# Interleaving the last three MLP block products by row tile, with row statistics on ScalarE and small steps on GpSimd

## The chip, the cores and the metric

The kernel runs on one core of a Trainium2 chip. Its engines are TensorE (matrix products into PSUM banks), VectorE, ScalarE and GpSimd (element work), and SyncE, which issues the transfers. Each engine works through a queue of its own in order and waits there for what other engines have to finish first. The metric is the device time of one execution in microseconds; less is better.

## The reference, cut to what matters

One inference step of a one-layer encoder over 1024 prompt rows and 64 sample rows, 1024 wide, in float32. What the change touches is its last line:

```
hdn = square(relu(x @ w_ff1))                          # hidden 4096
y   = layer_norm(alpha * x + hdn @ w_ff2, ln2_g, ln2_b)
layer_norm(x, g, b): mu = mean(x); var = mean((x - mu)**2)     # over the 1024 columns of a row
                     (x - mu) * rsqrt(var + 1e-5) * g + b
```

## The kernel before

The product `hdn @ w_ff2` is done as seven block products in the manner of Strassen and Winograd (P1 to P7) instead of eight, over four groups `g` of the hidden dimension. Each product is a step `s` of a group; each step has four row tiles `t` of 128 prompt rows, and one row tile is one call of `tile_mm`: twelve matmuls of 512 columns (four slices of the hidden dimension, each in three passes of split numbers) into one PSUM bank, then one VectorE instruction (L1306) that adds the bank into `acc`. This addition is called the eviction here. `acc[row]` holds the 1024 columns of row tile `row` (0 to 7; `NB` = 8 is the sample). `QUAD` says which half of the rows and which half of the columns a product belongs to.

Products share banks: P6, P7 and P4 go on accumulating in the bank that P1 began (`a0` to `a3`, one for each `t`), P3 in that of P5 (`b0` to `b3`). So P4 of a tile can't start before the eviction of P7 of the same tile has read the bank. In the last group the order of the steps is P1, P2, P6, P5, P3, P7, P4; steps 4, 5 and 6, that is P3, P7 and P4, finish the rows: rows 0 to 3 are complete after P3, rows 4 to 7 after P4.

TensorE's order is written by hand, here as a list of (step, tile). The order on the other engines is drawn up before the run by a planner that knows the instructions' inputs and estimates of their durations; it is fixed in the program.

`final(row)` normalises a complete row tile and writes it out. Its row statistics come from VectorE: `half_stats` (L1316) over each 512 columns, and an aggregate (L1373). `rstd_of` (L151 to L161) makes the reciprocal root: Ln and Exp on ScalarE, refined by four small VectorE steps on one column. For rows 0 to 5 and the sample, a further small step (L1384) makes the negated mean times root, ScalarE's Identity (L1388) writes the normalised half into a free `b` bank, VectorE multiplies by the gain (L1389), GpSimd adds the bias (L1390), SP issues the transfer. Rows 6 and 7 are done on VectorE alone, by two instructions over the row (L1376, L1379 in halves).

The sample's products (`sample_mm`) run between tiles, in banks `b0` or `b3`; `sample_sum` puts them together.

## Time and profile before

| what | us |
|---|---|
| median of 3 runs | 1297.64 |
| lowest and highest run | 1296.21, 1300.37 |
| the profiled execution | 1297.02 |
| its span, from the first to the last instruction | 1295.2 |
| TensorE busy in the span | 1209.0 (93%) |
| VectorE busy in the span | 952.1 (74%) |
| ScalarE, GpSimd busy in the span | 528.4 (41%), 107.0 (8%) |

Busy shares are means over the whole span. The change touches its last few per cent, so the views that count are those of single stretches there: busy time of each engine in a window, and the engines' timelines. Times in rows are microseconds from the start of the span, unless marked ns. PE is TensorE, PEld its weight loads, DVE VectorE, ACT ScalarE, POOL GpSimd, SPq SyncE's queue. A clock in a row is TensorE's granted clock as a share of 2.4 GHz.

### The profile page before, as it was taken

What the parts mean: (1) busy time and instruction counts of PE and PEld (TensorE: products, weight loads), DVE (VectorE), ACT (ScalarE), POOL (GpSimd) and SP (SyncE); (2) the same over time, 40 slices, a digit from 0 to 9 for tenths busy, and PEclk for the clock granted to TensorE, in tenths of its full rate; (3) what the DMA queues carried; (4) which work ended last, traced back from release to release, by engine and by line L of the source; (5) the groups of instructions that cost most, each with busy time, mean ns of one, the idle gap of its engine ahead of it and who ended that gap; (6) DMA issues with size and microseconds to landing.
All of it is one profiled execution on the core that took longest, in us unless ns stands there. A gap on an engine that the chain in (4) does not pass through costs nothing.

```text
span 1295.2 us, 18517 instructions
## 1 busy us (share of the span) xinstructions
PE 1209.0 (93%) x7162; PEld 1097.0 (85%) x7162; DVE 952.1 (74%) x1635; ACT 528.4 (41%) x1010; POOL 107.0 (8%) x57
## 2 busy tenths in 40 slices
PE   7989899989999799976999999999989999999994
PEld 5889789988899688865999999999978888888873
DVE  7855765866966687799776767676575688777888
ACT  4454464664664442223333333333434423323422
POOL 3130111111110010011000000000000000000013
PEclk9999899989999899987999999999989999999997
DMA  7771231222222443323535353542695545434203
GB/s 249 236 209 38 39 99 55 52 63 79 59 59 88 59 132 123 119 81 106 181 109 179 104 178 113 168 139 94 228 342 210 195 160 177 143 130 144 68 17 121
DMA packets 123234, 166.61 MB, mean 129 GB/s; under 512 B 13885, under 2 KB 90729, under 8 KB 119562
## 3 DMA queue, kind: packets, MB, share of 16 engines
q1 hardware_dynamic: 123146, 165.43, 40.6%
q8 instruction: 56, 0.92, 0.3%
q14 instruction: 32, 0.26, 0.1%
HBM read 112.20 MB, written 55.57 MB: 130 GB/s over the span
## 4 chain that ended last, share of the span: by engine, by line
PE 71%; DVE 16%; DMA 5%; ACT 4%; issue 4%; SPq 1%; DVEq 0%; POOL 0%; ACTq 0%; POOLq 0%
PE P L1299 19%; PE py L839 6%; PE fa L1001 5%; PE fa L999 5%; PE fa L997 5%; PE fc L999 2%; PE fc L997 2%; PE fc L1001 2%; PE v L480 1%; PE fb L999 1%; PE fb L997 1%; PE fb L1001 1%; DMA wo6r<-in_w_out 1%; PE t L644 1%; PE smP L1337 1%
## 5 line engine op out<-in xcount | busy, mean ns | idle before, releaser
L1299 PE MATMUL P<-wl,hh 128*128 128x512 f32 x448 | 175.7, 392 | 3.1 <-DVE wl L1150 3.1
L1299 PE MATMUL P<-wh,hh 128*128 128x512 f32 x448 | 175.6, 392 | 1.0 <-DVE sacc L1343 0.8
L1299 PE MATMUL P<-wh,hl 128*128 128x512 f32 x448 | 175.6, 392 | 0.0
L1299 PEld LDWEIGHTS P<-wl,hh 128*128 128x128 f32 x448 | 84.8, 189 | 21.2 <-DVE wl L1150 3.4
L1299 PEld LDWEIGHTS P<-wh,hh 128*128 128x128 f32 x448 | 84.8, 189 | 19.5 <-DVE sacc L1343 1.2
L1299 PEld LDWEIGHTS P<-wh,hl 128*128 128x128 f32 x448 | 84.8, 189 | 17.7
L1306 DVE TENSOR_TENSOR x<-x,P 128x512 f32<-128x512 f32 x96 | 64.4, 682 | 34.0 <-PE P L1299 33.7
L1148 ACT CAST hh<-hr 128x1024 fp32r<-128x1024 f32 (+1 forms) x28 | 37.2, 1359 | 110.2 <-PE P L1299 105.3
L997 PE MATMUL fc<-x,wP 128*128 128x272 f32 x248 | 71.6, 289 | 2.2 <-ACT x L203 2.2
L999 PE MATMUL fc<-x,wP 128*128 128x272 f32 x248 | 71.7, 289 | 0.8 <-DVE x L204 0.8
L1001 PE MATMUL fc<-x,wP 128*128 128x272 f32 x248 | 71.3, 288 | 0.0
L1390 POOL TENSOR_TENSOR x<-x 128x1024 f32<-128x1024 f32 x6 | 14.3, 2381 | 671.9 <-DVE n21v L156 656.9
L1150 DVE TENSOR_TENSOR hl<-hr,hh 128x1024 fp32r<-128x1024 f32 (+1 forms) x28 | 44.7, 1603 | 31.5 <-ACT hh L1148 31.5
L997 PEld LDWEIGHTS fc<-x,wP 128*128 128x128 f32 x248 | 46.7, 188 | 2.4 <-ACT x L203 2.4
L999 PEld LDWEIGHTS fc<-x,wP 128*128 128x128 f32 x248 | 46.8, 189 | 1.0 <-DVE x L204 1.0
L1001 PEld LDWEIGHTS fc<-x,wP 128*128 128x128 f32 x248 | 46.8, 189 | 0.0
L1001 PE MATMUL fa<-x,wP 128*128 128x272 f32 x128 | 38.1, 298 | 6.2 <-DVE wP L204 6.2
L619 PE MATMUL s<-kh,qs 128*128 128x512 f32 (+3 forms) x96 | 35.1, 369 | 7.0 <-DVE a20m L565 2.6
L1148 ACT CAST hh<-x 128x1024 fp32r<-128x1024 f32 (+1 forms) x13 | 17.6, 1384 | 53.3 <-PE P L1299 40.1
L997 PE MATMUL fa<-x,wP 128*128 128x272 f32 x128 | 38.0, 297 | 1.2 <-ACT wP L203 1.2
L999 PE MATMUL fa<-x,wP 128*128 128x272 f32 x128 | 37.8, 295 | 0.0
L203 ACT CAST x<-xt 128x512 fp32r<-128x512 f32 (+2 forms) x33 | 16.8, 545 | 49.2 <-PE xt L908 31.4
(1462 smaller groups left out, 3856.6 us busy)
## 6 DMA issues: line engine op xcount, KB each, us to landing
hr<-hv SPq DMA_DIRECT2D x19, 1024.0 KB, 4.9
hv<-hS SPq DMA_DIRECT2D x63, 256.0 KB, 4.4
w2B<-in_w_ff SPq DMA_DIRECT2D x11, 1024.0 KB, 5.7
hv<-hb SPq DMA_DIRECT2D x42, 256.0 KB, 2.9
x<-hv SPq DMA_DIRECT2D x9, 1024.0 KB, 5.5
f1r<-in_w_ff SPq DMA_DIRECT2D x17, 512.0 KB, 4.1
f1k<-in_w_ff SPq DMA_DIRECT2D x14, 512.0 KB, 4.9
x<-in_w_ff SPq DMA_DIRECT2D x6, 1024.0 KB, 7.6
```

Source lines behind the costliest of these rows:

```text
L203: nc.scalar.copy(out=hi, in_=src)
L480: nc.tensor.matmul(pv, lhsT=xx[:, k, off:off + 128], rhs=ww[:, k, :], start=(n == 0), stop=(n == len(ops) - 1))
L619: nc.tensor.matmul(p[:, c0:c1], lhsT=st, rhs=kh[:, m, c0:c1], start=True, stop=False)
L839: nc.tensor.matmul(py[:, s], lhsT=(ml if m == 2 else mh)[:, e, :], rhs=wo[e][m == 1][:, s], start=(n == 0), stop=(n == len(ops) - 1))
L997: nc.tensor.matmul(out, lhsT=w[:, 0, k, :], rhs=xh[:, k, cs], start=first and k == 0, stop=False, skip_group_check=not first)
L999: nc.tensor.matmul(out, lhsT=w[:, 0, k, :], rhs=xl[:, k, cs], start=False, stop=False, skip_group_check=not first)
L1001: nc.tensor.matmul(out, lhsT=w[:, 1, k, :], rhs=xh[:, k, cs], start=False, stop=last and k == 3, skip_group_check=not first)
L1148: nc.scalar.copy(out=hi[q], in_=src[:, w * q:w * q + w])
L1150: nc.vector.tensor_tensor(out=lo[q], in0=src[:, w * q:w * q + w], in1=f32(hi[q]), op=ALU.subtract)
L1299: nc.tensor.matmul(out, lhsT=x[f][:, c], rhs=w[f], start=new and f == 0 and n == 0, stop=f == GP - 1 and n == 2, skip_group_check=not new)
L1306: nc.vector.tensor_tensor(out=dst, in0=dst, in1=out, op=ALU.add)
L1390: nc.gpsimd.tensor_tensor(out=y[:rows], in0=y[:rows], in1=b, op=ALU.add)
```

## The change

Four things change. First, TensorE's list: P7 and P4 no longer follow all of P3, but the three steps are interleaved so that rows of the two halves become complete in turn; each (6,t) comes directly behind (5,t). `ready_rows` says after which tile which rows are normalised. Second, the rows below `SUMMED` = 6 no longer get statistics from `half_stats`: their evictions are made by `tensor_tensor_reduce`, which also gives the sum of each row, and ScalarE makes the squared deviations' sum by Square with a bias (the negated mean) and an accumulator. Third, the small one-column steps of these six rows and of the sample (`eng`) go to GpSimd; they lie as columns `c[n]` in one tile. Fourth, rows 6 and 7 keep `half_stats` and VectorE's small steps, but are now normalised by ScalarE's Identity too; their bias is added by GpSimd in halves (row 6) or by VectorE (row 7), and each half is written out by itself.

```diff
--- before.py
+++ after.py
@@ -1300,22 +1300,36 @@
                                      stop=f == GP - 1 and n == 2, skip_group_check=not new)
             half, dh = QUAD[p]
             dst = acc[4 * half + t][:, dh * 512:(dh + 1) * 512]
+            row = 4 * half + t
             if g == 0 and p in FIRST:
                 nc.scalar.copy(out=dst, in_=out)
+            elif g == NG - 1 and p in LAST_OF and row < SUMMED:
+                nc.vector.tensor_tensor_reduce(out=dst, in0=out, in1=dst, op0=ALU.add, op1=ALU.add, scale=1.0, scalar=0.0,
+                                               accum_out=col(row, dh))
             else:
                 nc.vector.tensor_tensor(out=dst, in0=dst, in1=out, op=ALU.add)
-            if g == NG - 1 and p in ("P2", "P7"):
-                half_stats(4 * half + t, dh)
+                if g == NG - 1 and p in LAST_OF:
+                    half_stats(row, dh)
+
+
+        LAST_OF = ("P2", "P3", "P7", "P4")
+        SUMMED = 6
+        kept2 = []
+
+        def stat_tile():
+            if not kept2:
+                kept2.append(f1a.tile([128, 1128], F32, name="n2st", tag="wx", bufs=2))
+            return kept2[0]
+
+        def col(t, n):
+            return stat_tile()[:, 128 + 16 * t + n:129 + 16 * t + n]
+
+        def stats_of(t):
+            return stat_tile()[:, 12 * t:12 * t + 12].rearrange("p (q c) -> p q c", q=2)
 
         def half_stats(t, q):
             rows = 128 if t < NB else SMP
-            if not stats2:
-                both = f1a.tile([128, 1128], F32, name="n2st", tag="wx", bufs=2)
-                for u in range(NB + 1):
-                    stats2[u] = both[:, 12 * u:12 * u + 12].rearrange("p (q c) -> p q c", q=2)
-            nc.vector.bn_stats(out=stats2[t][:rows, q, :], in_=acc[t][:rows, q * 512:(q + 1) * 512])
-
-        stats2 = {}
+            nc.vector.bn_stats(out=stats_of(t)[:rows, q, :], in_=acc[t][:rows, q * 512:(q + 1) * 512])
 
         def sample_sum(q):
 
@@ -1367,28 +1381,47 @@
             rows = 128 if t < NB else SMP
             dst = o["y_prompt"][0, t * 128:(t + 1) * 128, :] if t < NB else o["y_sample"][0]
             g, b = gb2[:rows, 0], gb2[:rows, 1]
-            if t < NB:
-                half_stats(t, 1 if t < 4 else 0)
-            mv = small([128, 2], f"n2{t}mv")
-            nc.vector.bn_aggr(out=mv[:rows], in_=stats2[t][:rows])
             halves = [slice(0, 512), slice(512, 1024)]
-            if t >= NB - 2 and t < NB:
-                nc.vector.scalar_tensor_tensor(out=y, in0=y, scalar=mv[:, 0:1], in1=g, op0=ALU.subtract, op1=ALU.mult)
-                r = rstd_of(mv[:, 1:2], rows, f"n2{t}")
-                for s in halves:
-                    nc.vector.scalar_tensor_tensor(out=y[:, s], in0=y[:, s], scalar=r, in1=b[:, s], op0=ALU.mult, op1=ALU.add)
+            if t < 4:
+                xn = [ps2.tile([128, 512], F32, name=f"xn{t}", tag=f"b{t}")] * 2
+            else:
+                xn = [ps2.tile([128, 512], F32, name=f"xn{t}{q}", tag=f"b{2 * (t == 6) + q}") for q in range(2)]
+            c = [col(t, n)[:rows] for n in range(16)]
+            late = SUMMED <= t < NB
+            eng = nc.vector if late else nc.gpsimd
+            if t < SUMMED:
+                eng.tensor_scalar(out=c[2], in0=c[0], scalar1=c[1], scalar2=-1.0 / D, op0=ALU.add, op1=ALU.mult)
+                for q, s in enumerate(halves):
+                    nc.scalar.activation(out=xn[q][:rows], in_=y[:rows, s], func=AF.Square, bias=c[2], scale=1.0,
+                                         accum_out=c[3 + q])
+                eng.tensor_scalar(out=c[5], in0=c[3], scalar1=c[4], scalar2=1.0 / D, op0=ALU.add, op1=ALU.mult)
+                var, mean, sign = c[5], c[2], 1.0
+            else:
+                mv = stat_tile()[:rows, 128 + 16 * t + 11:128 + 16 * t + 13]
+                nc.vector.bn_aggr(out=mv, in_=stats_of(t)[:rows])
+                var, mean, sign = mv[:, 1:2], mv[:, 0:1], -1.0
+            nc.scalar.activation(out=c[6], in_=var, func=AF.Ln, bias=eps[:rows], scale=1.0)
+            nc.scalar.activation(out=c[7], in_=c[6], func=AF.Exp, scale=-0.5)
+            eng.tensor_scalar(out=c[8], in0=var, scalar1=EPS, scalar2=None, op0=ALU.add)
+            eng.tensor_scalar(out=c[8], in0=c[8], scalar1=c[7], scalar2=c[7], op0=ALU.mult, op1=ALU.mult)
+            eng.tensor_scalar(out=c[8], in0=c[8], scalar1=-0.5, scalar2=1.5, op0=ALU.mult, op1=ALU.add)
+            eng.tensor_scalar(out=c[9], in0=c[8], scalar1=c[7], scalar2=None, op0=ALU.mult)
+            eng.tensor_scalar(out=c[10], in0=mean, scalar1=c[9], scalar2=sign, op0=ALU.mult, op1=ALU.mult)
+            for q, s in enumerate(halves):
+
+                nc.scalar.activation(out=xn[q][:rows], in_=y[:rows, s], func=AF.Identity, scale=c[9], bias=c[10])
+                if t == NB - 1:
+                    nc.vector.tensor_tensor(out=xn[q], in0=xn[q], in1=g[:, s], op=ALU.mult)
+                    nc.vector.tensor_tensor(out=y[:, s], in0=xn[q], in1=b[:, s], op=ALU.add)
+                else:
+                    nc.vector.tensor_tensor(out=y[:rows, s], in0=xn[q][:rows], in1=g[:, s], op=ALU.mult)
+                    if late:
+                        nc.gpsimd.tensor_tensor(out=y[:, s], in0=y[:, s], in1=b[:, s], op=ALU.add)
+                if late:
                     nc.sync.dma_start(out=dst[:, s], in_=y[:, s])
-                return
-            r = rstd_of(mv[:rows, 1:2], rows, f"n2{t}")
-            nmr = small([128, 1], f"n2{t}nm")
-            nc.vector.tensor_scalar(out=nmr[:rows], in0=mv[:rows, 0:1], scalar1=r[:rows], scalar2=-1.0, op0=ALU.mult, op1=ALU.mult)
-            for q, s in enumerate(halves):
-
-                xn = ps2.tile([128, 512], F32, name=f"xn{t}{q}", tag=f"b{t if t < 4 else 2 * (t % 2) + q}")
-                nc.scalar.activation(out=xn[:rows], in_=y[:rows, s], func=AF.Identity, scale=r[:rows], bias=nmr[:rows])
-                nc.vector.tensor_tensor(out=y[:rows, s], in0=xn[:rows], in1=g[:, s], op=ALU.mult)
-            nc.gpsimd.tensor_tensor(out=y[:rows], in0=y[:rows], in1=b, op=ALU.add)
-            nc.sync.dma_start(out=dst, in_=y[:rows])
+            if not late:
+                nc.gpsimd.tensor_tensor(out=y[:rows], in0=y[:rows], in1=b, op=ALU.add)
+                nc.sync.dma_start(out=dst, in_=y[:rows])
 
         steps = [(g, s) for g in range(NG) for s in range(7)]
         for n, (g, s) in enumerate(steps):
@@ -1414,17 +1447,14 @@
             if s in (0, 1, 5):
                 sample_mm(g, s)
         g = NG - 1
-        for s, t in ((4, 0), (4, 1), (4, None), (4, 2), (4, 3), (5, 0), (5, 1), (5, 2), (6, 0), (5, 3), (6, 1), (6, 2), (6, 3)):
+        ready_rows = {(4, None): (0, 1), (6, 0): (NB, 4), (4, 2): (2,), (6, 1): (5,), (4, 3): (3,), (6, 2): (6,), (6, 3): (7,)}
+        for s, t in ((4, 0), (4, 1), (4, None), (5, 0), (6, 0), (4, 2), (5, 1), (6, 1), (4, 3), (5, 2), (6, 2), (5, 3), (6, 3)):
             if t is None:
                 sample_mm(g, s)
-                final(0)
-                final(1)
-                continue
-            tile_mm(g, s, t)
-            if s == 6 or (s == 4 and t > 1):
-                final(t if s == 4 else 4 + t)
-            if (s, t) == (4, 3):
-                final(NB)
+            else:
+                tile_mm(g, s, t)
+            for row in ready_rows.get((s, t), ()):
+                final(row)
 
 
 _INS = ["x_prompt", "x_sample", "cache_k", "cache_v", "cache_conv", "ln0_g", "ln0_b", "rel_bias", "w_in", "conv_w",
```

## Rows read from the trace of the kernel before

**Rows 1.** By stretch: length; PE, PEld, DVE, ACT, POOL busy; clock; DMA share, GB/s

```profile
1237.00:1249.00 12.00, 10.42 (x45) 8.29 (x46) 9.61 (x13) 3.80 (x3) 0.00 (x0) 1.00 0.00 0
1249.00:1276.60 27.60, 27.58 (x121) 22.32 (x119) 25.84 (x70) 10.99 (x24) 12.02 (x5) 1.00 0.19 77
1276.60:1292.20 15.60, 0.00 (x0) 0.00 (x0) 14.29 (x27) 3.80 (x9) 4.68 (x2) 0.58 0.34 118
```

**Rows 2.** TensorE's timeline: start, us, engine, line, operation, tiles [idle before <-releaser]

```profile
1235.92 0.39 PE L1299 MATMUL P<-wh,hl 128*128 128x512 f32 x1
1237.07 0.50 PE L1299 MATMUL P<-wh,hh 128*128 128x512 f32 x1 [0.77 <-DVE sacc L1343]
...
1247.04 0.50 PE L1337 MATMUL smP<-wh,hs 128*128 128x512 f32 x1 [1.51 <-DVE x L1306]
...
1276.19 0.39 PE L1299 MATMUL P<-wh,hl 128*128 128x512 f32 x1
```

**Rows 3.** Timeline of VectorE, one eviction and the tail

```profile
1236.34 0.68 DVE L1343 TENSOR_TENSOR sacc<-sacc,smP 128x512 f32<-128x512 f32 x1
...
1275.61 1.64 DVE L1376 SCALAR_TENSOR_TENSOR x<-x,n26mv 128x1024 f32<-128x1024 f32 x1
...
1277.30 0.67 DVE L1306 TENSOR_TENSOR x<-x,P 128x512 f32<-128x512 f32 x1
1278.00 0.69 DVE L1316 BATCH_NORM_STATS2 n2st<-x 128x6 f32<-128x512 f32 x1
...
1279.86 0.20 DVE L1373 BATCH_NORM_AGGREGATE n27mv<-n2st 128x2 f32<-128x12 f32 x1
...
1280.24 3.14 DVE L1376 SCALAR_TENSOR_TENSOR x<-x,n27mv 128x1024 f32<-128x1024 f32 x1
...
1283.73 0.21 DVE L1384 TENSOR_SCALAR n25nm<-n25mv,n25q 128x1 f32<-128x1 f32 x1
1284.80 0.69 DVE L1389 TENSOR_TENSOR x<-xn,x 128x512 f32<-128x512 f32 x1 [0.85 <-ACT xn L1388]
...
1286.85 2.98 DVE L1379 SCALAR_TENSOR_TENSOR x<-x,n26q 128x512 f32<-128x512 f32 x2
...
1289.99 0.27 DVE L156 TENSOR_SCALAR n27v<-n27v,n27r 128x1 f32<-128x1 f32 x1
...
1290.74 1.42 DVE L1379 SCALAR_TENSOR_TENSOR x<-x,n27q 128x512 f32<-128x512 f32 x2
```

**Rows 4.** One line, an earlier normalisation: count: ns min/median/max, first and last start

```profile
L196 DVE SCALAR_TENSOR_TENSOR xn<-xn,n02q,b x1: 1285/1285/1285, 25.3 to 25.3; 128x1024 f32<-128x1024 f32 x1
```

**Rows 5.** Timeline of GpSimd in the tail

```profile
1279.97 2.34 POOL L1390 TENSOR_TENSOR x<-x 128x1024 f32<-128x1024 f32 x1 [3.80 <-DVE n25v L155]
1286.27 2.34 POOL L1390 TENSOR_TENSOR x<-x 128x1024 f32<-128x1024 f32 x1 [3.97 <-DVE x L1389]
```

**Rows 6.** VectorE by line, 1249.0 to 1292.2: count, busy us, mean ns, idle

```profile
L1316 DVE BATCH_NORM_STATS2 n2st<-x 128x6 f32<-128x512 f32 x10 | 6.9, 687 | 0.1
```

**Rows 7.** Line 565, an addition with a reduction, attention stage

```profile
L565 DVE CUSTOM_DVE_ANT_0 a03e<-s,bias x2: 693/693/693, 111.5 to 121.3; 128x512 f32<-128x512 f32 x2
L565 DVE DVE_READ_ACCUMULATOR2_ANT a03m<- x2: 83/84/84, 112.2 to 121.9; 128x1 f32 x2
```

**Rows 8.** Line 568, ScalarE's Exp with a sum, attention stage

```profile
L568 ACT ACTIVATE a03e<-a03e,a03m x2: 727/727/727, 112.3 to 122.1; 128x512 f32<-128x512 f32 x2
```

**Rows 9.** Timeline of ScalarE in the tail

```profile
1283.98 1.49 ACT L1388 ACTIVATE xn<-x,n25nm,n25q 128x512 f32<-128x512 f32 x2 [4.78 <-DVE n25nm L1384]
...
1285.50 0.28 ACT L151 ACTIVATE n27l<-n27mv,eps 128x1 f32<-128x1 f32 x1
1285.82 0.20 ACT L153 ACTIVATE n27r<-n27l 128x1 f32<-128x1 f32 x1
```

**Rows 10.** GpSimd by line, whole span: count, busy us, mean ns, idle before

```profile
masks.py:199 POOL TENSOR_SCALAR_AFFINE_SELECT ident<-ident 128x128 f32<-128x128 f32 x1 | 0.3, 285 | 0.0
...
L1457 POOL MEMSET const-float32-0.0<- 128x1 f32 x1 | 0.1, 99 | 0.2 <-issue 0.2
```

## The prediction

> **What bounds the kernel now.** I read the windows over the last 60 us first [rows 1], because the change touches only the end of the MLP's last group. From 1249.0 to 1276.6 TensorE is busy 27.58 of 27.60 us at a granted clock of 1.00 (2.4 GHz). Then it does nothing more, while VectorE is busy 14.29 of the next 15.60 us. So the end of this kernel is two bounds in a row: TensorE up to its last matmul, and behind it a VectorE backlog. The last matmul starts at 1276.19 and lasts 0.39, so it ends at 1276.58 [rows 2]; the last VectorE instruction ends at 1290.74 + 1.42 = 1292.16 [rows 3]; the span ends at 1295.2, 3.04 us later, with the last output transfers. Tail behind TensorE: 15.58 + 3.04 = 18.62 us.
>
> VectorE's own timeline of the tail says what the backlog is [rows 3]: row 7's eviction comes 0.7 us late (1277.30), its aggregate has to wait until 1279.86, its subtract-and-scale runs 3.14 us, then row 5's and row 6's work comes, and row 7's reciprocal root is refined only from 1289.99 on. Some of these are longer than the work: the same instruction form over 1024 columns took 1.28 in the earlier normalisations [rows 4], here 1.64 and 3.14, and the pair over 512 columns took 2.98 against 1.42 for the next pair. The 3.14 and the 2.98 lie across the GpSimd additions at 1279.97 and 1286.27 [rows 5]. About 3.8 us of the tail (0.36 + 1.86 + 1.56) is this slowing.
>
> TensorE's timeline shows two waits behind 1235, 0.77 and 1.51 us, both for a VectorE eviction that stood behind operand splits [rows 2]; none follows during the last ten tiles.
>
> **The change, part by part.**
> *Removed from VectorE after 1249.* Between 1249.0 and 1292.2 it is busy 25.84 + 14.29 = 40.1 us [rows 1]. The six summed rows lose their statistics; rows 6 and 7 keep four of the ten 0.687 us statistics in this stretch [rows 6], so 6 x 0.69 = 4.1 us go. The four two-operand instructions of rows 6 and 7 (1.64 + 3.14 + 2.98 + 1.42 = 9.2 us) go and come back as four products and two additions at 0.69 = 4.1 us [rows 3]. Seven rows move five small steps each to GpSimd: 35 x about 0.2 = 7 us of busy time, and six aggregates. Net some 17 us of 40: VectorE no longer has a backlog, and the new second inputs are in PSUM on one side, so the GpSimd slowing should go with it.
>
> *Evictions with a sum.* tensor_tensor_reduce is in the trace elsewhere: 0.693 us for 512 columns, 0.084 for the accumulator read behind it [rows 7], against 0.67 for the plain eviction at 1277.30 [rows 3]. At most +0.1 each.
>
> *ScalarE.* Each of six rows gets two Squares with a sum. The nearest row is the Exp with a sum over 512 columns, 0.727 [rows 8]; with its accumulator read I take 0.85, so 12 x 0.85 = 10 us, beside eighteen normalising passes, which were there before (a pair took 1.49 [rows 9]). ScalarE was busy 10.99 of 27.60 us [rows 1], so it has room: I cost the Squares at nothing, covered by TensorE's remaining tiles. Without that cover a row costs 1.7 us.
>
> *GpSimd.* Small steps: 7 for each of six rows and 5 for the sample, 47 in all; additions: seven of 2.4 us and two halves of 1.2, 19.2 us. The trace has no small arithmetic on GpSimd. Nearest from below: filling one column, 0.099 us; from above: the 128 x 128 select, 0.285 [rows 10], and far above them an addition, 2.34 [rows 5]. One column is nearest to the first two; I take 0.25 and 0.05 for the hand-over, 0.3. Then GpSimd has 47 x 0.3 + 19.2 = 33 us between 1247.1 and about 1282, nearly full but not the last. VectorE's own small steps took about 0.2 (0.27 and 0.21 in [rows 3]). The Trainium skill (GPSIMD Engine Reference, Engine selection) speaks against the move: it keeps elementwise work on VectorE and calls GpSimd about twice as slow for two inputs. By it a step would cost some 0.45 us (an estimate from that page's ratio), the queue 40 us, and it would end near 1287.5; no run here shows a small step there.
>
> *TensorE's order.* This is the part with a price on the path. P4 of a row tile accumulates in the bank that P7 leaves. Before, at least two tiles lay between (5,t) and (6,t), 5.5 us in which VectorE read the bank. Now all four (6,t) come directly behind (5,t), and the first matmul has to wait for that eviction. Queued behind it is everything that TensorE still has, so each wait moves the end. Its size from rows: the last matmul runs 0.39 where the next would have started 0.23 after it (+0.16); VectorE starts 0.02 later; from the eviction's start to the released matmul it was 0.73 (1236.34 to 1237.07); that matmul takes 0.50 in place of 0.39 (+0.11) [rows 2, 3]. Together 1.02, about 1.07 with an accumulator read. Four: 4.2 us, the lower bound. If each also finds VectorE inside a 0.6 us instruction: 6.6, the upper. VectorE will be some 70% busy (23 us of the 33 that TensorE now needs), so I add 0.7 x 0.3 = 0.2 each and take 5.0. (6,0) runs earlier than before, at 1252.8, but the splits that make its operands are the ones for which the eviction of (4,0), and with it TensorE at 1247.04, had to wait already [rows 2], so there is no new wait for them.
>
> *Row 7's tail.* From TensorE's last matmul, piece by piece [rows 3, 9]: start 0.02; eviction to statistics 0.70; statistics 0.70; aggregate and hand-over 0.22; Ln and Exp 0.52 (1285.50 to 1286.02) and 0.05 to VectorE; three refining steps 0.75 (1289.99 to 1290.74) and the negated mean 0.25 (1283.73 to 1283.98); Identity to the product 0.82 (1283.98 to 1284.80); two products and two additions 2.7. Sum 6.7 in place of 15.58. The transfers behind it stay at 3.04; there are still eleven of them on SP's queue, and row 7's stand behind those of rows 5, 3 and 6.
>
> *Sum.* 15.58 - 6.7 = 8.9 gained behind TensorE, 5.0 lost in it: 3.9 faster. The profiled execution took 1297.02 (its span and 1.82 around it), so 1293.1. The median of the runs before is 1297.64, 0.6 above that execution; against it the same gain gives 1293.7. I say 1293.2, nearer to the execution that the rows are from. With the waits between 4.2 and 6.6 the forecast's own range is 1292.3 to 1294.7, rounded out by the products' order in row 7 (0.6): 1291.7 to 1295.3.
>
> **The rivals.**
> *GpSimd becomes the bound (slower).* SP sends row 7's halves behind row 6's, which wait for GpSimd. If GpSimd runs without a gap from 1247.1, the end is 1247.1 + 19.2 + 47p + 3.04 + 1.82 = 1271.2 + 47p, where p is a small step with its hand-over. It passes 1297.0 at p = 0.55; at 0.65 it gives 1301.7. For it: dependent steps queue behind 2.4 us additions, and 33 of 35 us leaves no room; GpSimd's queue is in order. Against: the fill at 0.099 and the select at 0.285. The page above stands behind this rival; by its ratio p lies just under that point.
>
> *Products in front of evictions (same or slightly slower).* VectorE's order is fixed by a planner before the run. If it puts a product whose Identity hangs on GpSimd in front of P7's eviction, TensorE waits for a GpSimd addition: up to 2.4 us. Two of the four waits hit: 1293.2 + 4.8 = 1298. For it: before, VectorE had to wait for an Identity itself, 0.85 us at 1284.80 [rows 3], with only ScalarE between; GpSimd now enters this chain for the first time. Against: from 1252 to 1282 VectorE has a third of its time free.
>
> *The pair waits are hidden (much faster).* Then 8.9 us come whole: 1288.1. Only if the matmul needn't wait for the bank's reader; the 1.51 us wait for just such an eviction [rows 2] speaks against.
>
> *No effect.* TensorE ends about 5 us later and something else still ends at 1292: I see nothing that would, except the two cases above.
>
> **How the numbers follow.** Forecast 0.60, GpSimd as bound 0.12, products in front 0.20, hidden waits 0.08. A measurement of this kernel can tell about 0.3%, 3.9 us, from no change. The forecast's middle lies on that border: half of its 0.60 is faster, half is the same. Faster: 0.30 + 0.08 and a part of the runs that spread = 0.40. Same: 0.30 and half of the products' case = 0.40. Slower: 0.12 and the rest = 0.20. The range reaches down to halfway towards the hidden waits, 1289.5, and up over the products' case, 1299.0; outside are the rest of the hidden waits and GpSimd above 0.6 us a step.
>
> **What would show it.** In the profile after: four waits of TensorE for a VectorE eviction, 0.7 to 1.3 us each, and the last matmul near 1281.6; VectorE ending 6.7 us behind it; no VectorE instruction over 0.8 us behind 1250; a GpSimd small step near 0.25 us and its last addition before 1284; row 7's Identity started by VectorE's own step. The prediction is wrong if the first small GpSimd steps come late, if VectorE waits for ScalarE in front of an eviction, if row 7's transfers wait for row 6's, or if the granted clock falls in the four gaps (it stayed at 1.00 from 1237 to 1249 with 1.6 us idle [rows 1]).

## The result and the profile after

| | before | after |
|---|---|---|
| median, us (6 runs each, side by side) | 1296.93 | 1306.80 |
| lowest to highest | 1292.89 to 1300.37 | 1303.12 to 1309.52 |
| span of the profiled execution | 1295.2 | 1303.6 |
| sample's first matmul to TensorE's last | 29.5 | 47.9 |
| TensorE's last matmul to the span's end | 18.6 | 9.8 |

The ratio is 1.0075 (95% interval 1.0049 to 1.0102): slower by 0.75%, some 10 us; the prediction was 1293.2, in a range of 1289.5 to 1299.0. The last two rows of the table say where. The sample's first matmul is the third item of every list here, so it marks the same place in each kernel: 1247.04 before [rows 2], 1245.93 after. Behind TensorE 8.8 us were gained (8.9 predicted). In TensorE 18.3 us were lost (5.0 predicted).

TensorE's timeline of the kernel after (start, duration, engine, line, operation, shapes, and in brackets the idle time in front of it and what ended it), to set beside [rows 2]:

```profile
1245.93 0.50 PE L1351 MATMUL smP<-wh,hs 128*128 128x512 f32 x1 [1.52 <-DVE n2st L1307]
...
1266.85 0.79 PE L1299 MATMUL P<-wh,hh 128*128 128x512 f32 x1 [6.76 <-DVE n2st L1307]
...
1267.87 0.63 PE L1299 MATMUL P<-wh,hl 128*128 128x512 f32 x1
1268.30 0.63 PE L1299 MATMUL P<-wh,hh 128*128 128x512 f32 x1
...
1278.87 0.50 PE L1299 MATMUL P<-wh,hh 128*128 128x512 f32 x1 [0.78 <-DVE x L1310]
1279.21 0.39 PE L1299 MATMUL P<-wl,hh 128*128 128x512 f32 x1
1279.43 0.40 PE L1299 MATMUL P<-wh,hl 128*128 128x512 f32 x1
...
1289.17 0.50 PE L1299 MATMUL P<-wh,hh 128*128 128x512 f32 x1 [4.55 <-DVE x L1310]
...
1293.38 0.40 PE L1299 MATMUL P<-wh,hl 128*128 128x512 f32 x1
```

There are four waits for an eviction, as predicted, one at each P4 tile. Two have the predicted size: 0.78 idle and 0.27 for draining and restarting is 1.05 (the one at the first pair, not shown, has 0.79). Two are 6.76 and 4.55. The four idle times make 12.9 us, the four restarts 1.1.

The rest is in the matmuls: behind the 6.76 us gap they last 0.63 and start 0.43 apart, against 0.39 and 0.23 from 1279.21 on. The windows of the kernel after show why (length; busy time of PE, PEld, DVE, ACT, POOL; granted clock; DMA share, GB/s), beside [rows 1]:

```profile
1249.00:1259.20 10.20, 9.41 (x41) 7.41 (x40) 7.07 (x15) 6.27 (x15) 5.61 (x12) 1.00 0.00 1
1259.20:1266.00 6.80, 0.90 (x4) 0.40 (x3) 1.17 (x2) 2.00 (x3) 4.53 (x9) 0.75 0.38 154
1266.00:1273.00 7.00, 6.15 (x15) 4.85 (x16) 1.42 (x6) 4.48 (x14) 5.31 (x13) 0.51 0.19 40
1273.00:1279.00 6.00, 5.22 (x24) 4.00 (x23) 4.03 (x10) 4.57 (x12) 4.73 (x6) 1.00 0.22 87
...
1289.00:1293.80 4.80, 4.61 (x12) 3.32 (x12) 2.77 (x8) 1.48 (x2) 3.39 (x3) 0.64 0.31 125
```

In the gap and behind it the granted clock fell from 1.00 to 0.51, that is, from the 2.4 to the 1.2 GHz level, and came back to 1.00 by 1273; behind the second long gap it is 0.64 over the last tile. The tile at 1266.85 took 5.29 us to the start of the next, the one at 1278.87 2.87; with the slow start of the tile behind it (0.3) and the last tile's 4.61 in place of 3.04, the low clock cost 4.3 us. 12.9 + 1.1 + 4.3 = 18.3, the whole of TensorE's loss.

Also to be read in the windows: in the window in which TensorE did almost nothing (1259.2 to 1266.0), VectorE was busy 1.17 of 6.80 us and ScalarE 2.00. Neither was short of time. GpSimd, at 4.53, is the busiest. Why VectorE didn't read the bank is in its timeline, kernel after:

```profile
1258.32 0.19 DVE L1401 BATCH_NORM_AGGREGATE n2st<-n2st 64x2 f32<-64x12 f32 x1
1258.44 0.63 DVE L1307 CUSTOM_DVE_ANT_0 x<-P,x 128x512 f32<-128x512 f32 x1
1259.00 0.08 DVE L1307 DVE_READ_ACCUMULATOR2_ANT n2st<- 128x1 f32 x1
1264.81 1.39 DVE L1417 TENSOR_TENSOR acc<-xn,x 64x512 f32<-64x512 f32 x2 [5.73 <-ACT xn L1412]
1266.12 0.67 DVE L1307 CUSTOM_DVE_ANT_0 x<-P,x 128x512 f32<-128x512 f32 x1
...
1285.61 0.69 DVE L1417 TENSOR_TENSOR x<-xn,x 128x512 f32<-128x512 f32 x1 [1.71 <-ACT xn L1412]
1286.22 0.68 DVE L1310 TENSOR_TENSOR x<-x,P 128x512 f32<-128x512 f32 x1
...
1287.54 0.67 DVE L1417 TENSOR_TENSOR x<-xn,x 128x512 f32<-128x512 f32 x1
...
1288.44 0.68 DVE L1310 TENSOR_TENSOR x<-x,P 128x512 f32<-128x512 f32 x1
...
1293.82 0.69 DVE L1310 TENSOR_TENSOR x<-x,P 128x512 f32<-128x512 f32 x1 [1.12 <-PE P L1299]
...
1299.19 1.28 DVE L1415 TENSOR_TENSOR x<-xn,x 128x512 f32<-128x512 f32 x2
```

In VectorE's fixed order the sample's two products (64 rows, 1264.81) stand directly in front of the eviction of (5,1) at 1266.12. The bank was full at 1260.09 (1266.85 - 6.76), but VectorE stood at the products for 5.73 us, for ScalarE's Identity. In ScalarE's timeline the sample's Exp is done early, and its Identity waits for GpSimd's last step (L1409):

```profile
1258.88 0.20 ACT L1404 ACTIVATE n2st<-n2st 64x1 f32<-64x1 f32 x1
...
1264.00 1.48 ACT L1412 ACTIVATE xn<-acc,n2st 64x512 f32<-64x512 f32 x2 [4.92 <-POOL n2st L1409]
```

What held that step up is in GpSimd's timeline, kernel after:

```profile
1257.28 2.40 POOL L1423 TENSOR_TENSOR x<-x 128x1024 f32<-128x1024 f32 x1 [2.33 <-DVE x L1417]
1259.66 0.27 POOL L1393 TENSOR_SCALAR n2st<-n2st 128x1 f32<-128x1 f32 x1
1259.88 2.34 POOL L1423 TENSOR_TENSOR x<-x 128x1024 f32<-128x1024 f32 x1
1262.31 0.21 POOL L1405 TENSOR_SCALAR n2st<-n2st 64x1 f32<-64x1 f32 x1
1262.63 0.33 POOL L1406 TENSOR_SCALAR n2st<-n2st 64x1 f32<-64x1 f32 x1
1263.05 0.18 POOL L1407 TENSOR_SCALAR n2st<-n2st 64x1 f32<-64x1 f32 x1
1263.33 0.28 POOL L1408 TENSOR_SCALAR n2st<-n2st 64x1 f32<-64x1 f32 x1
1263.70 0.26 POOL L1409 TENSOR_SCALAR n2st<-n2st 64x1 f32<-64x1 f32 x1
```

The sample's variance was there at 1258.51 (VectorE's aggregate above), and its Exp ended at 1259.08. But GpSimd was inside row 0's addition of the bias, and had row 1's next in its queue; the sample's five steps began at 1262.31. They ended at 1263.96, the Identity ran from 1264.00, the products at 1264.81, the eviction at 1266.12. An idle VectorE, a full bank and an idle TensorE all waited behind two additions that nobody needed soon. Before, GpSimd's additions were the end of each row's chain; now its queue lies in the middle of it.

The second long wait is of another make. The bank of (5,3) was full at 1284.62 (1289.17 - 4.55). VectorE stood at a product until 1285.61, again for an Identity that hung on GpSimd's steps, and then did that product, the eviction of (6,2) (1286.22), statistics, a further product (1287.54), row 6's aggregate and its first small step before it came to this eviction at 1288.44. About 1 us of this wait is the late Identity, 2.8 us is VectorE's own work in front.

### The profile page after: what moved, and what is told of

It reads as the page before. It is cut to its first block, busy times and chain, and to the rows that moved or that the text cites. A ratio compares the mean times of both kernels' runs of the same rounds, so it can differ in the third digit from the quotient of the medians.

```text
span 1303.6 us, 18560 instructions
## 1 busy us (share of the span) xinstructions
PE 1211.8 (93%) x7162; PEld 1097.2 (84%) x7162; DVE 935.7 (72%) x1596; ACT 538.8 (41%) x1038; POOL 120.8 (9%) x106
## 4 chain that ended last, share of the span: by engine, by line
PE 68%; DVE 15%; DMA 6%; ACT 5%; issue 4%; POOL 1%; SPq 1%; DVEq 0%; ACTq 0%; POOLq 0%
PE P L1299 18%; PE py L839 6%; PE fa L999 5%; PE fa L997 5%; PE fa L1001 5%; PE fc L999 2%; PE fc L997 2%; PE fc L1001 2%; DMA w2B<-in_w_ff 1%; PE fb L999 1%; PE fb L997 1%; PE fb L1001 1%; DMA wo6r<-in_w_out 1%; PE v L480 1%; DVE wl L1150 1%
## 5 line engine op out<-in xcount | busy, mean ns | idle before, releaser
L1310 DVE TENSOR_TENSOR x<-x,P 128x512 f32<-128x512 f32 x84 | 56.3, 682 | 32.2 <-PE P L1299 32.1
L619 PE MATMUL s<-kh,qs 128*128 128x512 f32 (+3 forms) x96 | 34.5, 363 | 6.9 <-DVE a20m L565 2.6
L1148 ACT CAST hh<-x 128x1024 fp32r<-128x1024 f32 (+1 forms) x13 | 17.6, 1384 | 53.8 <-PE P L1299 40.1
L203 ACT CAST th<-t 128x512 fp32r<-128x512 f32 (+2 forms) x56 | 23.9, 428 | 32.2 <-PE t L644 27.3
```

Of the source, the lines that this page charges most:

```text
L203: nc.scalar.copy(out=hi, in_=src)
L619: nc.tensor.matmul(p[:, c0:c1], lhsT=st, rhs=kh[:, m, c0:c1], start=True, stop=False)
L1148: nc.scalar.copy(out=hi[q], in_=src[:, w * q:w * q + w])
L1310: nc.vector.tensor_tensor(out=dst, in0=dst, in1=out, op=ALU.add)
```

## The experiments

Three theories were set against each other. **Queues**: the loss comes from the in-order queues of GpSimd and VectorE, as just read, and goes when the small steps leave GpSimd. **Succession**: having (6,t) directly behind (5,t) in TensorE's list is what costs. **Steps**: the small steps, with their hand-overs between engines, are dear in themselves. Every kernel was timed beside the kernel before. The next table sorts the nine kernels that combine a list with a place for the statistics: ratio to before with its 95% interval, and from the profiled execution the stretch from the sample's first matmul to the span's end, in us.

| TensorE's list | statistics of before | of after, steps on GpSimd | of after, steps on VectorE |
|---|---|---|---|
| before's | 1; 48.2 | 1.0065 [1.0040, 1.0089]; 57.9 | 0.9959 [0.9941, 0.9977]; 43.2 |
| after's | 1.0017 [1.0003, 1.0031]; 50.6 | 1.0075 [1.0049, 1.0102]; 57.7 | 0.9974 [0.9955, 0.9994]; 45.5 |
| spread | 0.9992 [0.9975, 1.0008]; 48.2 | 1.0062 [1.0038, 1.0086]; 56.0 | 0.9944 [0.9922, 0.9965]; 41.3 |

Within a column, the list moves the time by 0.1 to 0.3%; within a row, the place of the small steps moves it by 1.0 to 1.2%, with every list. The differences of the stretches agree with the ratios (+9.5 us beside +0.75%, -6.9 beside -0.56%), so the effect lies in that stretch.

**The list alone** (list_only): before's statistics; the Identity of rows above 3 writes to banks that the new list leaves free.

```diff
-                xn = ps2.tile([128, 512], F32, name=f"xn{t}{q}", tag=f"b{t if t < 4 else 2 * (t % 2) + q}")
+                xn = ps2.tile([128, 512], F32, name=f"xn{t}{q}", tag=f"b{t if t < 4 else q}")
...
-        for s, t in ((4, 0), (4, 1), (4, None), (4, 2), (4, 3), (5, 0), (5, 1), (5, 2), (6, 0), (5, 3), (6, 1), (6, 2), (6, 3)):
...
+        for s, t in ((4, 0), (4, 1), (4, None), (5, 0), (6, 0), (4, 2), (5, 1), (6, 1), (4, 3), (5, 2), (6, 2), (5, 3), (6, 3)):
```

> Only TensorE's new list, with the finals of the kernel before (statistics, small steps and rows 6 and 7 on VectorE). Queue theory (VectorE's fixed order puts products that hang on GpSimd's chain in front of the evictions of P7, and TensorE stands behind them): no GpSimd step is in front of a product here, so each of the four waits stays under 2 us and the clock at 1.00; VectorE has its 40 us of work after 1249 as before, so the span is 1294 to 1298, ratio to before 0.998 to 1.003. Succession theory (P4 directly behind P7 is itself what costs the 17 us): TensorE's last matmul ends near 1290, span above 1302. Step theory (a small step on GpSimd is too dear): as the queue theory.

1297.81 us. TensorE waits 0.78, 0.85, 0.78 and 4.02 us at the four pairs, and its part of the stretch grows by 9.2 us (29.5 to 38.7); behind it 6.8 are given back. The time is as Queues expected, the last wait is not (under 2 us each, clock at 1.00): no GpSimd step stands in a chain here, but VectorE was busy with its own work for 4.00 of the 4.00 us from 1275.0 to 1279.0, and the clock over TensorE's last tile was 0.63. So this list does cost TensorE time, but little of it stays in the end. As the sole cause, the succession is ruled out.

**The statistics alone** (finals_only): all of the new `final` and the summed evictions, before's list.

```diff
+        ready_rows = {(4, None): (0, 1), (4, 2): (2,), (4, 3): (3, NB), (6, 0): (4,), (6, 1): (5,), (6, 2): (6,), (6, 3): (7,)}
+        for s, t in ((4, 0), (4, 1), (4, None), (4, 2), (4, 3), (5, 0), (5, 1), (5, 2), (6, 0), (5, 3), (6, 1), (6, 2), (6, 3)):
```

> The new finals and evictions with TensorE's old list. Queue theory: two tiles or more (5.5 us) lie between (5,t) and (6,t), so VectorE's waits for GpSimd's chain are mostly hidden from TensorE; last matmul at 1276 to 1279, VectorE's tail 6.7 us behind it unless GpSimd's 31 us end later; span 1286 to 1292, ratio 0.993 to 0.998. Succession theory: all 8.9 us of the tail come, span 1286 to 1288. Step theory: GpSimd's steps are the bound, it ends its last addition after 1290, span 1294 or more.

1305.77 us: as slow as the whole change. Queues and Succession had missed it; Steps had a span of 1294 or more and GpSimd's last addition after 1290 (it began at 1297.96). TensorE hardly waits here (1.8 us at one tile; last matmul 31.7 us behind the sample's first). The loss is behind TensorE, 26.3 us to the end. VectorE's timeline of this kernel:

```profile
1284.09 1.39 DVE L1417 TENSOR_TENSOR x<-xn,x 128x512 f32<-128x512 f32 x2 [7.61 <-ACT xn L1412]
1285.40 0.68 DVE L1307 CUSTOM_DVE_ANT_0 x<-P,x 128x512 f32<-128x512 f32 x1
...
1293.02 1.39 DVE L1417 TENSOR_TENSOR x<-xn,x 128x512 f32<-128x512 f32 x2 [5.17 <-ACT xn L1412]
```

What the Identity hangs on, GpSimd's timeline of the same kernel:

```profile
1271.91 2.35 POOL L1423 TENSOR_TENSOR x<-x 128x1024 f32<-128x1024 f32 x1 [2.33 <-DVE x L1417]
1274.22 2.40 POOL L1423 TENSOR_TENSOR acc<-acc,x 64x1024 f32<-64x1024 f32 x1
1276.59 2.40 POOL L1423 TENSOR_TENSOR x<-x 128x1024 f32<-128x1024 f32 x1
1278.97 0.26 POOL L1393 TENSOR_SCALAR n2st<-n2st 128x1 f32<-128x1 f32 x1
...
1285.57 2.35 POOL L1423 TENSOR_TENSOR x<-x 128x1024 f32<-128x1024 f32 x1 [2.33 <-DVE x L1417]
1287.89 0.27 POOL L1393 TENSOR_SCALAR n2st<-n2st 128x1 f32<-128x1 f32 x1
```

Here the loop stands open: three additions, then a row's first step (its negated mean, 1278.97), Squares on ScalarE, more steps, Identity, product (1284.09), that row's addition (1285.57), and only behind it the next row's first step (1287.89) and product (1293.02). 8.9 us a row, each engine waiting for most of it. So the queue theory had to be sharpened: the queues make a serial loop, and TensorE's list only decides whether TensorE stands inside the loop or VectorE comes late behind it.

**Evictions in front of the products** (evict_first): the Identities, and the products that hang on them, are held behind the eviction of a chosen P7 tile (`AFTER_P7`: tile to rows).

```diff
+        AFTER_P7 = {0: (0, 1), 1: (NB,), 2: (4, 2), 3: (5, 3)}
...
+            ctx = tc.issue_after(read_p7[-1].ins) if read_p7 else nullcontext()
+            ctx.__enter__()
             for q, s in enumerate(halves):
```

> The changed kernel, with the VectorE products of the sample put behind the eviction of tile (5,1), those of rows 4 and 2 behind that of (5,2), those of rows 5 and 3 behind that of (5,3); TensorE's list, GpSimd's work and all else as in the change. Queue theory: four waits of 0.8 to 1.5 us, granted clock 1.00 throughout, last matmul near 1281, span 1290 to 1295 (8 to 13 below the changed kernel), ratio to before 0.996 to 1.000. Succession theory: the waits stay, span above 1300. Step theory: TensorE ends early, but the rows' chains on GpSimd end as late as in the changed kernel (last addition near 1294), span 1300 or more.

1303.24 us, ratio 1.0051 [1.0032, 1.0071]. TensorE's timeline of this kernel at the second and the last pair:

```profile
1264.55 0.50 PE L1299 MATMUL P<-wh,hh 128*128 128x512 f32 x1 [0.79 <-DVE n2st L1307]
...
1284.74 0.80 PE L1299 MATMUL P<-wh,hh 128*128 128x512 f32 x1 [5.10 <-DVE x L1310]
```

VectorE's timeline of the same kernel, at the eviction that ends the last of these waits:

```profile
1280.42 0.68 DVE L1423 TENSOR_TENSOR acc<-xn,x 64x512 f32<-64x512 f32 x1 [4.82 <-ACT xn L1418]
...
1284.02 0.66 DVE L1310 TENSOR_TENSOR x<-x,P 128x512 f32<-128x512 f32 x1
```

And ScalarE's, where the Identity for that product stands:

```profile
1278.91 0.78 ACT L1418 ACTIVATE xn<-x,n2st 128x512 f32<-128x512 f32 x1 [1.57 <-POOL n2st L1412]
1279.63 1.47 ACT L1418 ACTIVATE xn<-acc,n2st 64x512 f32<-64x512 f32 x2
```

The 6.8 us wait is 0.79 now: VectorE's order made it. But the late products now stand in front of the last P7 eviction, and TensorE waits 5.10. The sample's last small step had ended at 1268.21; in ScalarE's fixed order its Identity stands behind that of another row, whose steps GpSimd finished at 1278.88. So ScalarE's queue is a third one in the loop, and no addition stood directly in front of those steps. An order on VectorE moves the lateness about; it doesn't remove it. The stretch is 53.7, 4.0 less than after. The run came out as Steps had it (span 1300 or more), not as Queues had it (1290 to 1295).

**No additions of the bias on GpSimd** (no_bias): rows 0 to 6 and the sample stay without their bias.

```diff
-                    if late:
-                        nc.gpsimd.tensor_tensor(out=y[:, s], in0=y[:, s], in1=b[:, s], op=ALU.add)
...
-                nc.gpsimd.tensor_tensor(out=y[:rows], in0=y[:rows], in1=b, op=ALU.add)
```

> The changed kernel without GpSimd's additions: the bias is left out of rows 0 to 6 and of the sample, the small steps stay on GpSimd. Queue theory (it is the 2.4 us additions in front of the small steps that make the chains late): the waits of 6.8 and 4.6 us shrink to under 2 us each, clock 1.00, last matmul 1281 to 1284, span 1290 to 1294. Step theory: 47 steps of 0.27 with their hand-overs still make the chains late, TensorE still waits 3 us or more at two tiles, span 1298 or more. Succession theory: unchanged, 1302.

1299.64 us, 1.0023 [1.0008, 1.0038]. The long waits are 3.36 and 3.62. The first had been 6.76, of which 3.5 were the additions by the reading above (Exp done at 1259.08, the step that uses it at 1262.63): 3.4 went, so for this wait the arithmetic closes. The rest of the expectation of Queues did not come true (waits under 2 us, span 1290 to 1294); that of Steps did (3 us or more at two tiles, span 1298 or more; it was 1298.5). In the second wait VectorE was busy with its own work for 3.12 of the 3.60 us from 1280.4 to 1284.0. The stretch is 52.1, 5.6 less than after.

**Small steps on VectorE** (steps_vector): one line, everything else as after.

```diff
-            eng = nc.vector if late else nc.gpsimd
+            eng = nc.vector
```

> The small steps of the statistics of rows 0 to 5 and of the sample go to VectorE (46 instructions of one column); the additions of the bias, and all else, stay as in the changed kernel. Theory of the interlocked queues (GpSimd's 2.34 us additions stand ahead of the small steps, and the products that hang on these steps stand ahead of evictions in VectorE's queue): the chain no longer passes GpSimd's queue, TensorE's two long waits (6.8 and 4.6 us) shrink to 1.5 us or less each, the granted clock stays 1.00, the last matmul ends near 1281 us and the span at 1289 to 1294 us, against 1303.6 of the changed kernel: ratio 0.991 to 0.998 of the kernel before. Theory that the succession of TensorE's tiles is to blame: as the changed kernel, waits of 10 us or more and a span over 1300 us. Rival, ScalarE's statistics with the hand-overs between engines are dear in themselves, on whichever engine the steps run: waits of 3 us or more stay in two places, as without the additions of the bias (3.4 and 3.6 us), and the span lies at 1296 to 1300 us.

1293.64 us. The prediction's waits are there now, 0.85, 0.79, 1.10 and 1.01; the clock is 1.00 as long as TensorE works, and it ends 34.5 us behind the sample's first matmul. VectorE's timeline of this kernel at the place of the former 6.8 us wait:

```profile
1262.19 0.69 DVE L1307 CUSTOM_DVE_ANT_0 x<-P,x 128x512 f32<-128x512 f32 x1 [0.90 <-PE P L1299]
1262.80 0.08 DVE L1307 DVE_READ_ACCUMULATOR2_ANT n2st<- 128x1 f32 x1
1262.80 1.31 DVE L1417 TENSOR_TENSOR acc<-xn,x 64x512 f32<-64x512 f32 x2
```

The eviction starts as soon as TensorE has filled the bank. The edit had a second effect: the planner drew up another order, with the sample's products behind the eviction of (5,1). The additions still run on GpSimd, 2.4 us each, and no step stands behind them.

**Order and additions, steps left on GpSimd** (no_bias_evict): to part the two effects, the two edits above in one kernel, evictions in front and no bias on rows 0 to 6 and the sample.

> The kernel with the evictions of P7 in front of the products, without GpSimd's additions of the bias (rows 0 to 6 and the sample stay without their bias); the small steps stay on GpSimd, and VectorE's order is that of the kernel with the evictions in front. If the long additions in GpSimd's queue and the order of VectorE make the whole loss: waits of TensorE of 0.8 us each, the last matmul 34 to 35 us behind the sample's first (as with the steps on VectorE), and a span of 1289 to 1295 us, ratio 0.993 to 0.998. If the small steps on GpSimd cost time of their own (1.3 times VectorE's duration, and two more hand-overs in each row's chain): a wait of 2 us or more stays at the last pair, and the span lies at 1296 to 1300 us, as without the additions alone (1298.5).

1296.01 us, 0.9994 [0.9981, 1.0008]. Waits of 0.79, 0.79, 0.78 and 2.34, the last matmul 35.4 us behind the sample's first, a span of 1297.1: within what was expected if the steps cost time of their own, and just outside the other expectation. The stretch is 48.1 against 45.5 with the steps on VectorE. So order and additions, 4.0 and 5.6 us each alone, make 9.6 together of the 12.2 us between those stretches (57.7 to 45.5); 2.6 stay with the steps on GpSimd, or with this forced order, which these runs don't part. So Steps, which named the outcome of several runs, isn't the main cause: with every step still on GpSimd four fifths of the loss go. Each stretch is that of one execution, and the intervals of the two ratios overlap, so the 2.6 is uncertain.

**Bias on VectorE, steps on GpSimd** (bias_vector):

```diff
...
-                    nc.vector.tensor_tensor(out=y[:rows, s], in0=xn[q][:rows], in1=g[:, s], op=ALU.mult)
...
+                nc.vector.tensor_tensor(out=xn[q][:rows], in0=xn[q][:rows], in1=g[:, s], op=ALU.mult)
+                nc.vector.tensor_tensor(out=y[:rows, s], in0=xn[q][:rows], in1=b[:, s], op=ALU.add)
...
-                nc.gpsimd.tensor_tensor(out=y[:rows], in0=y[:rows], in1=b, op=ALU.add)
```

> The small steps stay on GpSimd; the additions of the bias go to VectorE, in two halves of 512 columns behind each product, so that GpSimd's queue holds no long instruction in this stage (rows 0 to 5 and the sample; row 6 too). VectorE gets 14 halves of about 0.7 to 1.4 us more. Theory of the interlocked queues: as the run without the additions (1298.5 us span, waits of 3.4 and 3.6 us) plus what VectorE's work costs where it is the last, 0 to 4 us: 1296 to 1302 us, ratio 1.000 to 1.005, and less than half as good as moving the steps. Rival, the additions alone did the harm: waits of 1 us or less each and a span of 1293 us or less.

1303.49 us, 1.0059 [1.0037, 1.0081]: the ratio is just above the expected 1.000 to 1.005, the span (1299.9) inside 1296 to 1302. With nothing long in GpSimd's queue, waits of 1.9, 3.2 and 3.0 stay: for the last, VectorE's order now has eight halves of products and additions, from 1277.51 to 1282.41, in front of an eviction, and the first of them waited 2.97 us for an Identity. VectorE was busy through almost all of the three waits, so this run can't tell late steps from VectorE's added work.

**Before's list, steps on VectorE** (finals_vector): the edits of finals_only and steps_vector together.

> The last-row statistics of the changed kernel with the small steps on VectorE, and TensorE's tiles in the succession of the kernel before. Theory of the interlocked queues: without GpSimd in the chain, the loop of a row (product, addition, next row's small step) is broken, and VectorE comes to its last eviction within about 4 us of TensorE's end instead of 15; TensorE ends near 1277 to 1279 us, the tail behind it is near 7 to 12 us, and the span is 1286 to 1294 us: ratio 0.989 to 0.998. If it was the succession of TensorE's tiles alone that counted: 1286 to 1292 us, which the run with the steps on GpSimd (1306.0 us) has already contradicted. Rival of dear hand-overs: 1298 us or more, VectorE waiting for ScalarE's Identity for 3 us and more at each row.

1290.39 us. No wait at any P4 tile; TensorE needs 29.5 us, as before; VectorE ends 8.8 us behind its last matmul.

**The spread list**: one more tile between (5,t) and (6,t), with each of the three statistics; `ready_rows` follows the list. First with the steps on VectorE (spread_vector):

```diff
-        for s, t in ((4, 0), (4, 1), (4, None), (5, 0), (6, 0), (4, 2), (5, 1), (6, 1), (4, 3), (5, 2), (6, 2), (5, 3), (6, 3)):
+        for s, t in ((4, 0), (4, 1), (4, None), (5, 0), (4, 2), (6, 0), (5, 1), (4, 3), (6, 1), (5, 2), (5, 3), (6, 2), (6, 3)):
```

> As the run with the small steps on VectorE, but with one more tile between the last P7 and the last P4 tile of a row pair wherever the list has room, so that an eviction has about 2.75 us more before its P4 tile asks for the bank. Theory of the interlocked queues: what is left of the waits (about 0.8 us in two to four places with the steps on VectorE) falls to under 0.8 us at all but the last two tiles; the span is 0 to 2 us shorter than with the steps on VectorE alone, 1288 to 1293 us. Theory of the succession: the spread is what helps, and the gain over the steps on VectorE alone is 3 us or more.

1287.39 us, the lowest median of this study, 0.56% under the kernel before. The gain over steps_vector (0.3%, 4 us in the stretch) is more than the queue theory had expected; this point goes to the succession, though the two intervals overlap and the size is uncertain. Its windows, to set beside [rows 1]:

```profile
1249.00:1277.90 28.90, 28.85 (x127) 23.36 (x125) 25.16 (x86) 22.47 (x53) 13.32 (x6) 1.00 0.23 82
1277.90:1285.70 7.80, 0.00 (x0) 0.00 (x0) 7.39 (x20) 3.88 (x9) 5.84 (x4) 0.82 0.42 168
```

TensorE is busy 28.85 of 28.90 us, and VectorE ends 7.8 us behind it in place of 15.6: this is the kernel that the change was taken for.

The same list with before's statistics (spread_only, with the banks of list_only):

> The kernel before with the list that keeps one more tile between P7 and P4, and with nothing of the new statistics. Theory of the interlocked queues: the statistics of before hang on VectorE alone, so TensorE waits little (under 2 us in all), its last matmul ends near 1278 us, but VectorE still has all its work and ends 11 to 15 us behind TensorE: 1290 to 1297 us, ratio 0.995 to 1.001, at best half of the gain of the version with the small steps on VectorE. If the list is what made that version fast: 1285 to 1290 us.

1294.64 us with before's statistics: the list by itself is worth nothing that can be told from no change, as expected.

The same list with the steps on GpSimd (spread_steps_gpsimd):

> The changed kernel (small steps on GpSimd) with the list that keeps one more tile between P7 and P4. Theory of the interlocked queues: TensorE's waits shrink somewhat, but the chain of a row through GpSimd sets the end, as it did with the succession of before (1306.0 us span): 1299 to 1307 us, ratio 1.002 to 1.009, 10 us or more over the same list with the steps on VectorE (1289.6). If the list is what made that version fast: within 3 us of it, 1287 to 1293 us.

1304.01 us with the steps on GpSimd: as expected, the list doesn't help there (waits of 5.2 and 3.5).

And with row 6 summed too (spread_plus):

> The list with one more tile between P7 and P4 and the small steps on VectorE, with row 6 too summed by its evictions and squared on ScalarE: two statistics passes of 0.68 us fewer on VectorE, two Squares with their reads (1.74 us) more on ScalarE. If VectorE sets the end of that version (it is 9.7 of 10 us busy between 1270 and 1280): 0.5 to 1.5 us shorter, 1287 to 1289 us span. Rival: row 6's chain gets longer by its Squares and ends last: 0 to 2 us longer.

With `SUMMED` = 7 (row 6 too by sums and Squares) on the spread list and the steps on VectorE: 1289.99 us, 0.9954 [0.9935, 0.9972]. Not to be told from spread_vector; the stretch is 41.9 beside 41.3.

## Why the prediction was wrong

**Behind TensorE: the number right, in part by luck.** From the last matmul's end (1293.78) to VectorE's last end (1300.47) 6.69 us, predicted 6.7; the transfers 3.13 behind, predicted 3.04. Of VectorE's 40.1 us 26.9 are left (sum of the windows from 1249.0 to 1300.5); I had removed 17 and it was 13. But finals_only, with the same statistics and a TensorE that hardly waits, has VectorE 23.2 us behind the last matmul (1279.75 to 1302.90): with the steps on GpSimd the 6.7 came out only because TensorE itself ended late. With the steps on VectorE and no wait of TensorE (spread_vector) it is 7.8.

**Prices of the single instructions: right.** Eviction with a sum 0.63 to 0.69 and 0.08, Square 0.67 and 0.19 for its read (0.85 predicted). Of the eighteen normalising passes only fourteen were there before, those of rows 0 to 5 and of the sample; ScalarE got four more, 0.75 each. GpSimd by line, kernel after, between 1240 and 1306 (count, busy us, mean ns, idle before):

```profile
L1423 POOL TENSOR_TENSOR x<-x 128x1024 f32<-128x1024 f32 x6 | 14.3, 2377 | 4.5 <-DVE x L1417 4.5
...
L1406 POOL TENSOR_SCALAR n2st<-n2st 128x1 f32<-128x1 f32 (+1 forms) x7 | 2.4, 336 | 3.7 <-ACT n2st L1404 3.6
...
L1409 POOL TENSOR_SCALAR n2st<-n2st 128x1 f32<-128x1 f32 (+1 forms) x7 | 1.9, 266 | 0.6
```

The 47 small steps took 13.2 us (0.28 each), the additions 19.2: 32.4, predicted 33. A dependent step follows 0.28 to 0.42 us behind the one before it. The same lines on VectorE (steps_vector) have means of 266 ns for L1406 and 203 for L1409: GpSimd takes 1.3 times as long. The Trainium skill (GPSIMD Engine Reference, Engine selection) keeps elementwise work on VectorE and names a factor of about two for two inputs; the same row of its table puts one-input work at roughly line rate. The small steps have one tile as input and scalars of a row beside it, so the prediction's 0.45 took the wrong half of that row; measured is 1.3. The two-input additions bear the factor out: 2.38 on GpSimd for 1024 columns, 1.28 on VectorE for two halves (L1415). Its advice holds here, and the one-line move back is worth 1%; but the price lay in the queue more than in the rate.

**GpSimd's place in the chain: the assumption behind the miss.** I costed GpSimd by the sum of its work, found it "nearly full but not the last", and left it off the path. Its last addition began at 1292.07, not before 1284, though it was idle for 14.7 of the 44.8 us between 1249.0 and 1293.8. A sum of busy time bounds an engine from below; it doesn't show how long a chain takes that enters its queue three times a row, behind instructions eight times as long as its own. The Squares, costed at nothing under TensorE's cover, lie in that chain too: in the open loop of finals_only they are 1.6 of the 8.9 us (1279.27 to 1280.88).

**TensorE's order: the step that failed.** Its term was 5.0 us (bounds 4.2 and 6.6) for four waits for an eviction. The undisturbed wait was priced rightly (1.05 against 1.02 to 1.07). The total was 18.3, because the upper bound allowed an eviction only one 0.6 us instruction in front of it on VectorE, and no wait inside VectorE's queue. The rival "products in front of evictions" had the mechanism and even the number of waits hit, two of four; I gave it 0.20 and a price of one addition, 2.4 us each. Their excess over 0.78 was 6.0 and 3.8: in the first, two additions, five steps, an Identity and a pair of products in a row; in the second, a late Identity and 2.8 us of VectorE's own work. A wait of VectorE for ScalarE in front of an eviction was among the signs that I had named. My argument against it, that VectorE has a third of its time free, was no argument: VectorE was idle for 5.73 us and couldn't go on.

**The clock.** Named as something that would make the prediction wrong, and left out of every sum. 4.3 us.

**GpSimd as the bound by a full queue: not what happened.** With p = 0.37, from the distances of dependent steps above, its formula gives 1271.2 + 47 x 0.37 = 1288.6; the profiled execution took 1305.43, 17 us more. It was the time that a chain spends in GpSimd's queue, not GpSimd's load.

**Open.** What of the last 2.6 us is the steps' own length on GpSimd, what the two more hand-overs in each row's chain, what VectorE's order.

## What to carry to other kernels

Before moving small steps to an idle engine, look at what else stands in that engine's queue, and count the chain that passes it in order of time, not the engine's busy sum: one short step behind a 2.4 us instruction costs up to 2.4 us to all who wait for it. Where orders are fixed beforehand, look for the instruction in front of each eviction that releases TensorE, and ask which engine it hangs on. If two parts of a change pull opposite ways, time them apart: here the new statistics with their steps on VectorE gave 0.4 to 0.5% with each list, and the steps' move to GpSimd took away more than twice that.

## What the runs showed of the hardware

TensorE's granted clock stayed at 1.00 across idle times of 0.8 to 1.5 us between busy stretches, and fell behind single gaps of 6.76 and 4.55 us: 0.51 from 1266 to 1273, 0.64 from 1289.0 to 1293.8. It fell only after the restart in the second case (the matmul at 1289.51 lasts 0.40, those from 1290.03 on 0.63). A long wait is paid for twice: here 4.3 us on top of 11.3.

The length of the gap alone doesn't settle it. In the experiments the clock fell behind gaps of 3.36 us (no_bias, 0.50 from 1263.9 to 1267.0), 4.02 (list_only, 0.63 over the last tile) and 5.10 (evict_first, 0.61 over the last tile). It also fell behind one of only 1.94 us in bias_vector (0.83 from 1260.1 to 1270.2, the matmuls from 1260.96 on last 0.63), but stayed at 1.00 behind one of 2.34 us in no_bias_evict (1281.3 to 1284.4, matmuls of 0.39 to 0.40).
